# Wider pad tiles, another term order in the out projection, and three projection chunks issued ahead of the layer's sums

## Chip, core and metric

The kernel runs on one core of a Trainium2 chip. The metric is the device time of one execution in microseconds (us), as the median of several executions.

## What is computed

The input x has 512 tokens of 1024 channels. Two blocks of two layers each follow one another; all is float32. Cut to what matters:

```python
def hybrid_layer(x, ...):                        # block 1, twice
    proj = rmsnorm(x, norm_g) @ w_in             # 1024 -> 3584, split in 15 parts
    y_a = conformer_conv(a_u, a_v, ...) * silu(a_z)    # 31 taps, then layer norm
    y_b = short_gated_conv(b_b, b_c, b_x, conv_b_w) * silu(b_z)
    y_c = window_gqa(c_q, c_k, c_v, swa_sink) * silu(c_z)
    y_d = neighborhood_attn(d_q, d_k, d_v, na_rpb) * silu(d_z)
    return x + concat(y_a, y_b, y_c, y_d) @ w_out
x = rms_norm(x, final_norm_g)
for l in range(2):                               # block 2
    proj = rms_norm(x, g_mix) @ w_in             # pool, q, kv, lru and gate parts
    x = x + (g0 * pool + g1 * mla + g2 * lru) @ w_out   # each branch has its projection
    x = x + square(relu(rms_norm(x, g_ffn) @ w_ff1)) @ w_ff2   # 1024 -> 4096 -> 1024
return rms_norm(x, g_final)
```

## The kernel before

Activations lie transposed: a tile is 128 channels by 512 tokens, and x is eight such tiles. Every product with a weight matrix is made in chunks of 128 output channels. `weights` (line 136) loads a chunk (128 x 1024) by DMA on SP's queue into one of two raw tiles and splits it into a high part whi (ACT, line 125) and a low part wlo (DVE, line 126), each with three buffers, so that the split runs up to two chunks ahead of PE. The activations are split in the same way (xh and xl, hh and hl, fh and fl, yh and yl), and `mm3` (line 148) adds three products for each of the eight 128-channel terms: high by high (line 152), high by low (153) and low by high (154). A chunk is so 24 matmuls of 512 columns. `gemm` (line 156) takes a PSUM bank for it from the tag mm, which has three; the attention has banks of its own, two with tag sc for the scores and one with tag o for the output; the remaining two, tag t, serve transposes, sums (ss) and spreads (sp).

The RMS norm is put off: the chunks are made of x times the norm's weights, and the factor R (a token's reciprocal root) is multiplied in when DVE drains a bank (lines 330 to 333, names cq, ck, cv, av, au, kl, ql, kr, qr). R itself comes in a chain: the squares of x's eight tiles are added up (sqa, line 231), PE sums them over the channels (ss, line 169), DVE makes the root in some fourteen steps on 128x4 numbers (lines 175 to 193), spreads it to two diagonal tiles dh and dl (lines 197 and 199), PE multiplies these by ones (sp, lines 200 and 201) and ACT copies R out of the bank (rstd, line 203). No drain of a layer's first projection can start before that. At the end of block 1 there are two such factors: R, and R1, by which DVE multiplies the eight tiles of x (lines 645 and 646). In block 2 the two key and value chunks (kl) and the three query chunks (ql) have norms of their own (Rk and Rq, lines 694 and 700), by the same chain.

What the SBUF pool lays out stands in the order of first use, each tag in as many buffers as it names: the weights, x, hl, work and small tiles first, then three pad tiles (used by the convolutions, the pooling and the LRU part), and behind them hc (the convolution's sums), prob and pth (attention) and sixteen gate tiles. The split activations xh, hh, yh and wfh are hl tiles; fh and fl, the FFN's hidden part, and mh and ml, the merged branches, are gate tiles.

In each engine the instructions stand in an order that the Tile scheduler sets when the program is built, from the order of the code and its own estimate of what is ready; each engine then goes through its own list and waits where an operand isn't there yet. In the layers of block 1, `Side.beside` (line 377) puts the projections between the steps of the attention, and two of the 30 taps of each of two convolutions with every step. The out projection (lines 624 to 633) makes eight chunks over y[0] to y[7], in this order of terms; y[0] and y[1] (`finish_a`, line 593) are the last to be done, as they wait for the layer norm behind the taps. The mixing projection of block 2 (line 882), the two FFN products (lines 897 and 907) and the last projection (line 940) have the same form; in the last, fh is the stationary operand and wfh and wfl the moving ones.

The lines that the change touches, as they stand before:

```python
625            p = gemm(g["w_out"][l, m], y)
...
635        v1 = mean_eps(token_sums(sq.parts()), D)
...
916            R = rstd_of(sq.parts(), D)
```

## Time and profile before

| | us |
|---|---|
| median of 3 executions | 1956.35 |
| lowest and highest | 1953.57, 1956.74 |
| profiled execution | 1955.09 |
| its span in the trace | 1953.3 |

| engine | busy us | share of the span |
|---|---|---|
| PE (matmul) | 1905.2 | 98% |
| DVE | 1208.0 | 62% |
| ACT | 831.7 | 43% |
| POOL | 68.6 | 4% |

The profiled execution takes 1.8 us more than its span, before the first and behind the last recorded instruction. PE is a pipeline, so the duration of one matmul (some 390 ns) overlaps the next; what a matmul costs is read from start to start. The clock that TensorE was granted is shown as a share of full speed, 1.00 for 2.4 GHz and 0.50 for 1.2 GHz.

### The profile page before, as it was taken

To read this page: it belongs to the slowest core of one execution; us is meant where nothing else is said; L and a number is where in the kernel's file an instruction comes from. 1 tells how busy PE (TensorE), PEld (TensorE's weight loads), DVE (VectorE), ACT (ScalarE), POOL (GpSimd) and SP (SyncE) were. 2 spreads that over 40 slices of the span, in tenths; PEclk is the share of its full clock that TensorE was granted. 3 is DMA by queue.
4 is the path that set the end of the run, shared out by engine and by line. 5 is a ranking of instruction groups with operands and counts; after the bars stand their busy time and mean duration, and the time that the engine had idled before them with its cause. 6 is when DMAs were issued, how large, how long until landed. Compare 5 with 4: busy or idle time off the path is not lost.

```text
span 1953.3 us, 23068 instructions
## 1 busy us (share of the span) xinstructions
PE 1905.2 (98%) x8866; PEld 1526.3 (78%) x8866; DVE 1208.0 (62%) x2127; ACT 831.7 (43%) x1343; POOL 68.6 (4%) x83
## 2 busy tenths in 40 slices
PE   7999999999998999999999999999999999999998
PEld 6887778877776788888888888766788888888886
DVE  8997579976787545564444446786455564444454
ACT  7565355654367533343232234367433343323242
POOL 0000100002100000020000001000000010000001
PEclk9999999999999999999999999999999999999999
DMA  5232231222212123323333233221133323333341
GB/s 193 75 97 82 93 102 65 95 76 88 79 58 69 65 87 97 96 88 98 97 96 95 91 97 98 75 79 65 65 97 97 96 87 97 97 92 97 92 129 44
DMA packets 53678, 175.21 MB, mean 90 GB/s; under 512 B 6208, under 2 KB 10176, under 8 KB 53568
## 3 DMA queue, kind: packets, MB, share of 16 engines
q1 hardware_dynamic: 53568, 173.74, 28.1%
q8 instruction: 70, 1.15, 0.2%
q14 instruction: 40, 0.33, 0.1%
HBM read 171.62 MB, written 2.10 MB: 89 GB/s over the span
## 4 chain that ended last, share of the span: by engine, by line
PE 90%; ACT 4%; DVE 4%; issue 2%; DMA 0%; SPq 0%; ACTq 0%; DVEq 0%
PE mm L152 25%; PE mm L153 25%; PE mm L154 25%; PE o L315 2%; PE t L235 2%; PE br L154 1%; PE br L153 1%; PE br L152 1%; PE sc L745 1%; PE sc L440 1%; ACT whi L125 1%; DVE wlo L126 1%; PE last L154 1%; PE last L153 1%; PE last L152 1%
## 5 line engine op out<-in xcount | busy, mean ns | idle before, releaser
L125 ACT ACTIVATE whi<-raw 128x1024 fp32r<-128x1024 f32 (+2 forms) x314 | 320.9, 1023 | 798.6 <-PE mm L153 596.8
L126 DVE TENSOR_TENSOR wlo<-raw,whi 128x1024 fp32r<-128x1024 f32 (+2 forms) x314 | 369.2, 1176 | 169.6 <-ACT whi L125 168.8
L152 PE MATMUL mm<-xh,whi 128*128 128x512 f32 x992 | 396.4, 400 | 9.7 <-ACT whi L125 8.7
L154 PE MATMUL mm<-xh,wlo 128*128 128x512 f32 x992 | 393.7, 397 | 2.3 <-DVE wlo L126 2.2
L153 PE MATMUL mm<-xl,whi 128*128 128x512 f32 x992 | 392.8, 396 | 0.0
L152 PEld LDWEIGHTS mm<-xh,whi 128*128 128x128 f32 x992 | 187.5, 189 | 51.6 <-ACT whi L125 10.8
L154 PEld LDWEIGHTS mm<-xh,wlo 128*128 128x128 f32 x992 | 187.4, 189 | 44.3 <-DVE wlo L126 4.9
L153 PEld LDWEIGHTS mm<-xl,whi 128*128 128x128 f32 x992 | 187.7, 189 | 39.0 <-issue 3.3
L153 PE MATMUL mm<-hl,whi 128*128 128x512 f32 x512 | 199.4, 390 | 0.0
L152 PE MATMUL mm<-hh,whi 128*128 128x512 f32 x512 | 199.2, 389 | 0.0
L154 PE MATMUL mm<-hh,wlo 128*128 128x512 f32 x512 | 199.2, 389 | 0.0
L154 PE MATMUL mm<-fh,wlo 128*128 128x512 f32 x448 | 177.0, 395 | 0.0
L152 PE MATMUL mm<-fh,whi 128*128 128x512 f32 x448 | 176.9, 395 | 0.0
L153 PE MATMUL mm<-fl,whi 128*128 128x512 f32 x448 | 176.9, 395 | 0.0
L909 DVE TENSOR_TENSOR ff<-mm,rstd 128x512 f32<-128x512 f32 x56 | 38.8, 692 | 148.3 <-PE mm L154 148.3
L152 PEld LDWEIGHTS mm<-hh,whi 128*128 128x128 f32 x512 | 96.1, 188 | 20.0
L154 PEld LDWEIGHTS mm<-hh,wlo 128*128 128x128 f32 x512 | 96.1, 188 | 19.9
L153 PEld LDWEIGHTS mm<-hl,whi 128*128 128x128 f32 x512 | 96.1, 188 | 19.9
L332 DVE TENSOR_TENSOR lg<-mm,rstd 128x512 f32<-128x512 f32 x48 | 33.1, 690 | 126.8 <-PE mm L154 126.7
L154 PEld LDWEIGHTS mm<-fh,wlo 128*128 128x128 f32 x448 | 84.1, 188 | 20.4
L153 PEld LDWEIGHTS mm<-fl,whi 128*128 128x128 f32 x448 | 84.1, 188 | 20.4
L152 PEld LDWEIGHTS mm<-fh,whi 128*128 128x128 f32 x448 | 84.1, 188 | 20.3
(302 smaller groups left out, 2754.4 us busy)
## 6 DMA issues: line engine op xcount, KB each, us to landing
raw<-in_w_in SPq DMA_DIRECT2D x124, 512.0 KB, 3.3
raw<-in_w_ff SPq DMA_DIRECT2D x120, 512.0 KB, 3.6
raw<-in_w_out SPq DMA_DIRECT2D x32, 512.0 KB, 3.4
raw<-in_w_br SPq DMA_DIRECT2D x16, 512.0 KB, 3.6
raw<-in_w_last SPq DMA_DIRECT2D x8, 512.0 KB, 3.8
raw<-in_w_q SPq DMA_DIRECT2D x12, 192.0 KB, 2.3
x<-in_xT SPq DMA_DIRECT2D x8, 256.0 KB, 6.6
bends<-in_rpb SPq DMA_DIRECT2D x8, 256.0 KB, 4.5
```

Of the source, the lines that this page charges most:

```text
L125: A.activation(hi, src, AF.Copy)
L126: V.tensor_tensor(lo, src, hi.bitcast(F32), op=ALU.subtract)
L152: T.matmul(out, lhsT=wh, rhs=xh, start=(first and i == 0), stop=False)
L153: T.matmul(out, lhsT=wh, rhs=xl, start=False, stop=False)
L154: T.matmul(out, lhsT=wl, rhs=xh, start=False, stop=(last and i == n - 1))
L235: T.matmul(out, lhsT=in_, rhs=ident, is_transpose=True, start=True, stop=True)
L315: T.matmul(out[64 * j : 64 * j + 64, i * P : (i + 1) * P], lhsT=v(b), rhs=t[:, at[j, e]], start=(b == keys[i][0]), stop=(b == keys[i][1] - 1))
L332: V.tensor_tensor(t, p, R, op=ALU.mult)
L440: T.matmul(out, lhsT=q[j][:, i * P : (i + 1) * P], rhs=k[j][part][:, b0 * P : b1 * P], start=(part == 0), stop=(part == 1))
L745: T.matmul(out, lhsT=q[h][:, i * P : (i + 1) * P], rhs=kt[h][:, b0 * P : b1 * P], start=True, stop=True)
L909: V.tensor_tensor(t, p, Rf2, op=ALU.mult)
```

## The change

1. The pad tiles have 576 columns in place of 542 (seven places in the code, of which the diff shows two); what is written and read of them stays, but the two memsets behind the data in `conv_a`'s part now cover 49 columns instead of 15.
2. The out projection of block 1 adds its terms in the order y4, y5, y2, y6, y7, y3, y0, y1.
3. At the end of both layers of block 1 and of the first layer of block 2, a new function `ahead` issues three chunks of the next layer's projection before the sums that R needs. Their banks are the two of tag sc and the one of tag o, which the attention doesn't use then. The first two chunks are made of the first seven terms each and then of their last one, as x's last tile is the last to be done. `proj` takes these banks where the chunks are asked for: CQ, CQ + 1 and CK in block 1, the two kl chunks and the first ql chunk in block 2.
4. The sums and the root for the FFN's norm (Rf2) move from ahead of the FFN loop to behind its second chunk.

```diff
@@ -153,13 +153,25 @@
             T.matmul(out, lhsT=wh, rhs=xl, start=False, stop=False)
             T.matmul(out, lhsT=wl, rhs=xh, start=False, stop=(last and i == n - 1))
 
-    def gemm(dram, xs):
+    def gemm(dram, xs, order=None):
 
         kk = len(xs)
         h, l = weights(dram, kk, P)
         out = mmps()
-        mm3(out, [((h[:, k, :], l[:, k, :]), xs[k]) for k in range(kk)])
+        mm3(out, [((h[:, k, :], l[:, k, :]), xs[k]) for k in order or range(kk)])
         return out
+
+    def ahead(drams, xs, banks):
+
+        outs = [bank() for bank in banks]
+        ws = [weights(d, KD, P) for d in drams[:2]]
+        for ks in (range(KD - 1), range(KD - 1, KD)):
+            for out, (h, lo) in zip(outs, ws):
+                for k in ks:
+                    mm3(out, [((h[:, k, :], lo[:, k, :]), xs[k])], k == 0, k == KD - 1)
+        h, lo = weights(drams[2], KD, P)
+        mm3(outs[2], [((h[:, k, :], lo[:, k, :]), xs[k]) for k in range(KD)])
+        return outs
 
     def token_sums(parts):
 
@@ -483,7 +495,7 @@
             t = work("avt")
             A.activation(t, v, AF.Tanh, scale=0.5)
             u = scaled(proj(AU + c), R, "au")
-            pad = ap_.tile([P, S + 30], F32, tag="pad", name=uniq("pad"), bufs=3)
+            pad = ap_.tile([P, S + 64], F32, tag="pad", name=uniq("pad"), bufs=3)
             G.memset(pad[:, :15], 0.0)
             G.memset(pad[:, S + 15 :], 0.0)
             V.scalar_tensor_tensor(pad[:, 15 : S + 15], t, 1.0, u, op0=ALU.add, op1=ALU.mult)
@@ -622,7 +634,7 @@
         sqf = SumSq() if last else None
         nxs = []
         for m in range(KD):
-            p = gemm(g["w_out"][l, m], y)
+            p = gemm(g["w_out"][l, m], y, (4, 5, 2, 6, 7, 3, 0, 1))
             V.scalar_tensor_tensor(x[m], p, 0.5, x[m], op0=ALU.mult, op1=ALU.add)
             sq.add(x[m])
             if last:
@@ -632,6 +644,8 @@
             else:
                 nxs.append(split_tile(x[m], col("norm_g", l + 1, m), "x"))
         xs = nxs
+        cs = (CQ, CQ + 1, CK) if not last else (5, 6, 2)
+        first = dict(zip(cs, ahead([g["w_in_2"][0, c] if last else g["w_in"][l + 1, c] for c in cs], xs, (scps, scps, ops))))
         v1 = mean_eps(token_sums(sq.parts()), D)
         if not last:
             R = spread(rsqrt(v1))
@@ -680,7 +694,7 @@
         bd = {(n, c): bdt[:, 2 * i + c, :] for i, n in enumerate(HEADED) for c in range(2)}
 
         def proj(c):
-            return gemm(g["w_in_2"][l, c], xs)
+            return first.pop(c) if c in first else gemm(g["w_in_2"][l, c], xs)
 
 
         cos, sin = gate("cos"), gate("sin")
@@ -883,11 +897,8 @@
             V.scalar_tensor_tensor(x[m], p, 0.5, x[m], op0=ALU.mult, op1=ALU.add)
             sq.add(x[m])
             hs.append(split_tile(x[m], col("g_ffn_2", l, m), "h"))
-        rf = rsqrt(mean_eps(token_sums(sq.parts()), D))
-        V.tensor_tensor(rf, rf, rf, op=ALU.mult)
-        Rf2 = spread(rf)
-
-
+
+        sums = sq
         sq = SumSq()
         nxs = []
         last = l == DEPTH - 1
@@ -901,6 +912,10 @@
                 hi, lo = gate("fh", dt=F32R), gate("fl", dt=F32R)
                 split(t, hi, lo)
                 f.append((hi, lo))
+                if qt == 0 and c == 1:
+                    rf = rsqrt(mean_eps(token_sums(sums.parts()), D))
+                    V.tensor_tensor(rf, rf, rf, op=ALU.mult)
+                    Rf2 = spread(rf)
             if last and qt == 3:
                 break
             for m in range(KD):
@@ -913,12 +928,13 @@
                     nxs.append(split_tile(x[m], col("g_mix_2", l + 1, m), "x"))
         if not last:
             xs = nxs
+            first = dict(zip((5, 6, 2), ahead([g["w_in_2"][l + 1, c] for c in (5, 6, 2)], xs, (scps, scps, ops))))
             R = rstd_of(sq.parts(), D)
 
 
     gf = []
     for h in range(2):
-        t = ap_.tile([P, S + 30], F32, tag="pad", name=uniq("gf"), bufs=3)[:, :S]
+        t = ap_.tile([P, S + 64], F32, tag="pad", name=uniq("gf"), bufs=3)[:, :S]
         nc.sync.dma_start(out=t, in_=g["g_final"][:, h * S : (h + 1) * S].to_broadcast([P, S]))
         gf.append(t)
     ss = small("ssh")
```

The scheduler makes of this other lists for the engines. Four places follow, before and then after (a line of after stands 12 to 16 lower in its file than the same line of before). PE, start of layer 0's out projection; yh_1949 and yl_1950 are y0, yh_1991 and yl_1992 are y1, mm_2001, mm_2039 and mm_2077 the first three chunks. Before:

```order
L152 MATMUL mm_2077<-yh_1949,whi_2073 128x512
L153 MATMUL mm_2077<-yl_1950,whi_2073 128x512
L154 MATMUL mm_2077<-yh_1949,wlo_2074 128x512
L152 MATMUL mm_2001<-yh_1991,whi_1997 128x512
L152 MATMUL mm_2039<-yh_1991,whi_2035 128x512
L152 MATMUL mm_2077<-yh_1991,whi_2073 128x512
L153 MATMUL mm_2001<-yl_1992,whi_1997 128x512
L154 MATMUL mm_2001<-yh_1991,wlo_1998 128x512
L152 MATMUL mm_2001<-yh_1206,whi_1997 128x512
```

After:

```order
L152 MATMUL mm_2001<-yh_1907,whi_1997 128x512
L153 MATMUL mm_2001<-yl_1908,whi_1997 128x512
L154 MATMUL mm_2001<-yh_1907,wlo_1998 128x512
L152 MATMUL mm_2001<-yh_1949,whi_1997 128x512
L153 MATMUL mm_2001<-yl_1950,whi_1997 128x512
L154 MATMUL mm_2001<-yh_1949,wlo_1998 128x512
L152 MATMUL mm_2001<-yh_1991,whi_1997 128x512
L153 MATMUL mm_2001<-yl_1992,whi_1997 128x512
L154 MATMUL mm_2001<-yh_1991,wlo_1998 128x512
```

The terms of y0 and y1 came ahead of the others of their chunk, with three chunks open at once; now they close each chunk, and one chunk is done before the next begins.

PE, start of layer 1 of block 1, where the transposes of cv (t_2539) stand; cv's own chunk is mm_2512, mm_2552 is av's, mm_2587 au's and mm_2626 the second av's. Before:

```order
L154 MATMUL mm_2552<-xh_2067,wlo_2549 128x512
L152 MATMUL mm_2552<-xh_2107,whi_2548 128x512
L153 MATMUL mm_2552<-xl_2108,whi_2548 128x512
L235 MATMUL t_2539<-c_ident,cv_2537 128x128 x4
L154 MATMUL mm_2552<-xh_2107,wlo_2549 128x512
L152 MATMUL mm_2552<-xh_2147,whi_2548 128x512
L153 MATMUL mm_2552<-xl_2148,whi_2548 128x512
```

After:

```order
L152 MATMUL mm_2587<-xh_2307,whi_2583 128x512
L153 MATMUL mm_2587<-xl_2308,whi_2583 128x512
L154 MATMUL mm_2587<-xh_2307,wlo_2584 128x512
L247 MATMUL t_2539<-c_ident,cv_2537 128x128 x4
L152 MATMUL mm_2626<-xh_2029,whi_2622 128x512
L153 MATMUL mm_2626<-xl_2030,whi_2622 128x512
```

The transposes stood inside av's chunk, one chunk behind cv's; now they stand behind cv's, av's and au's, which hold all three mm banks, and the chunk that follows takes cv's bank again.

PE, start of block 2; sp_4730 before and sp_4761 after spread Rk. Before:

```order
L152 MATMUL mm_4829<-xh_4405,whi_4825 128x512
L153 MATMUL mm_4829<-xl_4406,whi_4825 128x512
L200 MATMUL sp_4730<-dh_4731,ones_r 128x512
L154 MATMUL mm_4829<-xh_4405,wlo_4826 128x512
L152 MATMUL mm_4829<-xh_4450,whi_4825 128x512
L153 MATMUL mm_4829<-xl_4451,whi_4825 128x512
L201 MATMUL sp_4730<-dl_4732,ones_r 128x512
L154 MATMUL mm_4829<-xh_4450,wlo_4826 128x512
```

After:

```order
L152 MATMUL mm_4921<-xh_4495,whi_4917 128x512
L153 MATMUL mm_4921<-xl_4496,whi_4917 128x512
L181 MATMUL ss_4737<-ones,sqa_4735 128x1 x4
L154 MATMUL mm_4921<-xh_4495,wlo_4918 128x512
L212 MATMUL sp_4761<-dh_4762,ones_r 128x512
L213 MATMUL sp_4761<-dl_4763,ones_r 128x512
L152 MATMUL mm_4969<-xh_4184,whi_4965 128x512
```

The two spreads stood inside a chunk, with its matmuls ahead of and between them; now a single matmul stands between the sums ss_4737 and the spread.

DVE, start of block 2; x_67 to x_74 are x, rstd_4580 and rstd_4673 are R1, kl the two key chunks, and sqa feeds the sums for Rk. Before:

```order
L126 TENSOR_TENSOR wlo_4826<-raw_4823,whi_4825 128x1024
L646 TENSOR_TENSOR x_67<-x_67,rstd_4580 128x512
L646 TENSOR_TENSOR x_68<-x_68,rstd_4580 128x512
L646 TENSOR_TENSOR x_69<-x_69,rstd_4580 128x512
L646 TENSOR_TENSOR x_70<-x_70,rstd_4580 128x512
L646 TENSOR_TENSOR x_71<-x_71,rstd_4580 128x512
L646 TENSOR_TENSOR x_72<-x_72,rstd_4580 128x512
L646 TENSOR_TENSOR x_73<-x_73,rstd_4580 128x512
L646 TENSOR_TENSOR x_74<-x_74,rstd_4580 128x512
L332 TENSOR_TENSOR kl_4700<-mm_4675,rstd_4548 128x512
L126 TENSOR_TENSOR wlo_4918<-raw_4915,whi_4917 128x1024
L231 TENSOR_TENSOR sqa_4704<-sq_4667,sq_4702 128x512
```

After:

```order
L344 TENSOR_TENSOR kl_4731<-sc_4500,rstd_4641 128x512
L660 TENSOR_TENSOR x_67<-x_67,rstd_4673 128x512
L660 TENSOR_TENSOR x_68<-x_68,rstd_4673 128x512
L660 TENSOR_TENSOR x_69<-x_69,rstd_4673 128x512
L660 TENSOR_TENSOR x_70<-x_70,rstd_4673 128x512
L660 TENSOR_TENSOR x_71<-x_71,rstd_4673 128x512
L660 TENSOR_TENSOR x_72<-x_72,rstd_4673 128x512
L660 TENSOR_TENSOR x_73<-x_73,rstd_4673 128x512
L660 TENSOR_TENSOR x_74<-x_74,rstd_4673 128x512
L243 TENSOR_TENSOR sqa_4735<-sq_4729,sq_4733 128x512
```

The eight multiplications by R1 stood between the two kl drains; now they stand behind both and ahead of sqa.

## Rows read from the trace of the kernel before

**Rows 1.** The page, part 1: busy us (share of the span) xinstructions, by engine.

```profile
PE 1905.2 (98%) x8866; PEld 1526.3 (78%) x8866; DVE 1208.0 (62%) x2127; ACT 831.7 (43%) x1343; POOL 68.6 (4%) x83
```

**Rows 2.** Groups by line: line, engine, operation, out<-in, xcount | busy us, mean ns.

```profile
L152 PE MATMUL mm<-hh,whi 128*128 128x512 f32 x512 | 199.2, 389 | 0.0
...
L154 PE MATMUL mm<-fh,wlo 128*128 128x512 f32 x448 | 177.0, 395 | 0.0
...
L154 PE MATMUL mm<-mh,wlo 128*128 128x512 f32 x128 | 50.6, 395 | 0.0
```

**Rows 3.** Timeline of PE (start us, us) where fh begins, hh begins, fh begins.

```profile
914.71 0.40 PE L152 MATMUL mm<-fh,whi 128*128 128x512 f32 x1
...
959.50 0.39 PE L152 MATMUL mm<-hh,whi 128*128 128x512 f32 x1
...
1003.03 0.40 PE L152 MATMUL mm<-fh,whi 128*128 128x512 f32 x1
```

**Rows 4.** PE's waits: who waited for whom: us in total, times, longest us.

```profile
PE ss L169 <- DVE sqa L231: 4.3, 2, 3.3
```

**Rows 5.** Timeline of PE, start of the out projections of layer 0 and 1 (idle in brackets).

```profile
208.21 0.39 PE L152 MATMUL mm<-yh,whi 128*128 128x512 f32 x1
...
210.60 0.50 PE L154 MATMUL mm<-yh,wlo 128*128 128x512 f32 x1 [0.42 <-DVE wlo L126]
212.59 1.03 PE L152 MATMUL mm<-yh,whi 128*128 128x512 f32 x3 [1.49 <-ACT yh L125]
...
213.90 0.63 PE L154 MATMUL mm<-yh,wlo 128*128 128x512 f32 x1
214.32 0.63 PE L152 MATMUL mm<-yh,whi 128*128 128x512 f32 x1
...
455.39 0.49 PE L154 MATMUL mm<-yh,wlo 128*128 128x512 f32 x1 [0.42 <-DVE wlo L126]
457.38 0.97 PE L152 MATMUL mm<-yh,whi 128*128 128x512 f32 x3 [1.50 <-ACT yh L125]
```

**Rows 6.** Busy time by stretch: us, PE, PEld, DVE, ACT, POOL (xcount), PEclk, DMA share, GB/s.

```profile
213.40:216.80 3.40, 3.40 (x9) 2.71 (x9) 0.00 (x0) 0.00 (x0) 0.00 (x0) 0.50 0.00 0
506.90:513.80 6.90, 6.90 (x21) 5.75 (x22) 3.33 (x15) 1.06 (x1) 0.00 (x0) 0.51 0.07 29
296.00:386.00 90.00, 89.91 (x493) 73.26 (x493) 87.28 (x171) 54.23 (x118) 0.25 (x3) 1.00 0.27 87
```

**Rows 7.** Timeline of DVE, PE and ACT at the layer end of block 1.

```profile
256.05 0.69 DVE L626 SCALAR_TENSOR_TENSOR x<-mm,x 128x512 f32<-128x512 f32 x1 [1.60 <-PE mm L154]
...
264.23 1.22 DVE L126 TENSOR_TENSOR wlo<-raw,whi 128x1024 fp32r<-128x1024 f32 x1
...
292.78 0.69 DVE L332 TENSOR_TENSOR au<-mm,rstd 128x512 f32<-128x512 f32 x1 [3.30 <-PE mm L154]
...
258.94 1.02 PE L169 MATMUL ss<-ones,sqa 128*128 128x1 f32 x8
...
282.99 0.66 PE L235 MATMUL t<-c_ident,cv 128*128 128x128 f32 x4 [1.56 <-DVE cv L332]
...
264.90 0.60 ACT L203 ACTIVATE rstd<-sp 128x512 f32<-128x512 f32 x1 [1.36 <-PE sp L201]
...
269.69 5.14 ACT L247 ACTIVATE rot<-cq 32x512 f32<-32x512 f32 x8
```

**Rows 8.** Timeline of ACT and DVE at the end of block 1.

```profile
517.80 0.60 ACT L203 ACTIVATE rstd<-sp 128x512 f32<-128x512 f32 x1 [4.55 <-PE sp L201]
...
522.23 4.89 DVE L646 TENSOR_TENSOR x<-x,rstd 128x512 f32<-128x512 f32 x8
...
560.64 0.69 DVE L332 TENSOR_TENSOR qr<-mm,rstd 128x512 f32<-128x512 f32 x1 [2.06 <-PE mm L154]
```

**Rows 9.** Timeline of DVE at the layer end of block 2.

```profile
1234.59 0.69 DVE L332 TENSOR_TENSOR kl<-mm,rstd 128x512 f32<-128x512 f32 x1
...
1277.57 0.69 DVE L332 TENSOR_TENSOR qr<-mm,rstd 128x512 f32<-128x512 f32 x1
```

More of the change, by code (lines that the diff above doesn't have):

```diff
@@ L551, in conv_b @@
             cb = scaled(proj(BC + c), R, "bc")
-            pad = ap_.tile([P, S + 30], F32, tag="pad", name=uniq("padb"), bufs=3)
+            pad = ap_.tile([P, S + 64], F32, tag="pad", name=uniq("padb"), bufs=3)
             G.memset(pad[:, :1], 0.0)
@@ L759, in pool @@
         def pool(c):
-            pu = ap_.tile([P, S + 30], F32, tag="pad", name=uniq("padp"), bufs=3)
+            pu = ap_.tile([P, S + 64], F32, tag="pad", name=uniq("padp"), bufs=3)
             G.memset(pu[:, :16], 0.0)
@@ L768, in pool @@
             while w < wins[1]:
-                nxt = ap_.tile([P, S + 30], F32, tag="pad", name=uniq("padd"), bufs=3)
+                nxt = ap_.tile([P, S + 64], F32, tag="pad", name=uniq("padd"), bufs=3)
                 G.memset(nxt[:, :16], 0.0)
@@ L791, in lru_in @@
         def lru_in(c):
-            pu = ap_.tile([P, S + 30], F32, tag="pad", name=uniq("padl"), bufs=3)
+            pu = ap_.tile([P, S + 64], F32, tag="pad", name=uniq("padl"), bufs=3)
             G.memset(pu[:, :3], 0.0)
@@ L812, in lru_in @@
             A.activation(tr, tr, AF.Tanh)
-            a2 = ap_.tile([P, S + 30], F32, tag="pad", name=uniq("a2"), bufs=3)[:, :S]
+            a2 = ap_.tile([P, S + 64], F32, tag="pad", name=uniq("a2"), bufs=3)[:, :S]
             A.activation(a2, a, AF.Square)
```

## The prediction

> **What bounds the kernel now.** I read the page first: PE is busy 98% of the span, 1905.2 of 1953.3 us, and no other engine two thirds of it [rows 1]. So the time is the sum of PE's matmuls plus the few stretches in which PE stands still or runs at the lower clock, and a change can only pay in three ways: a cheaper matmul, a wait less, a clock drop less. Next I looked at what one matmul costs [rows 2], then start to start in time order [rows 3], since a duration of 389 ns overlaps the next one: the 192 matmuls of one FFN quarter over hh, hl run from 959.50 to 1003.03, 226.7 ns each; the 192 over fh, fl from 914.71 to 959.50, 233.3 ns each. The shape, the weights' tiles and the clock are the same. Then PE's waits [rows 4]; by places the largest that the change touches are the two out projections of block 1 [rows 5], the layer end of block 1 [rows 7] and the end of block 1 (3.3 us [rows 4]). Last I looked at the granted clock by stretches [rows 6]: after some of these waits PE is granted 0.50, the 1.2 GHz level. A matmul then takes 427 ns start to start (213.90 to 214.32 [rows 5]), so the 3.4 us stretch costs 3.4 x (1 - 227/427) = 1.6 us and a 6.8 us stretch 3.2 us.
>
> **Wider pads.** The pads' contents are the same, and the reads of them too. What moves is what the pool lays out behind them. Three pads of 542 floats take 3 x 2176 bytes (rounded up), 25.5 times 256; so gate, hc, prob and pth tiles, which come later, start at a multiple of 256 bytes, while whi, wlo, hl, work and x start 128 bytes off one. Three pads of 576 floats take 27 times 256, and all start 128 off. The rows split just so: matmuls that pair a weight tile with an hl tile (hh) have a mean of 389 ns, those that pair one with a gate tile (fh, mh) 395 [rows 2]; the last projection pairs fh and wfh, a gate and an hl tile, in the same way. Whether the distance of the two operands decides or where the one starts, the new layout puts every pair where the fast ones stand, and I take 226.7 ns for all. One quarter is worth 44.79 - 43.53 = 1.26 us [rows 3]. There are 7 quarters over fh (3 x 448 matmuls), mh and ml make 2 more (3 x 128), the last projection 1 (3 x 64): 10 x 1.26 = **12.6 us**. Bounds: 0 if the place in memory is not the cause, 12.6 if it is wholly; I take the upper, because the step at 914.71 and back at 959.50 falls on the very matmul where the tile changes. The four memsets that grow from 15 to 49 columns are on POOL, which is 4% busy [rows 1]: 0.
>
> A rule of the Trainium skill speaks against this part. Its page "TensorE: Matmul & The Clock Gate" (section "Step-by-step: what each phase is for") says that PE reads the moving operand and the next weights through two read ports that don't take bandwidth from each other, so the tile that is streamed should not matter, this term would be 0 and the sum 1958.9 us. The trace does not agree as it stands: 6.6 ns per matmul go with the tile and with nothing else that I find [rows 3].
>
> **Order of the out projection.** y0 and y1 end last: zz of y1 is split into yh and yl on ACT and DVE while PE has started [rows 5]. Before, PE took the y0 terms of three chunks, waited 0.42 for the third chunk's wlo and 1.49 for y1, and was then granted half the clock. After, six finished terms come first: 18 matmuls x 0.227 = 4.1 us from 208.21, so y0 is wanted at 212.3 and y1 at 213.0; the yh that ended the wait let PE go at 212.59, and yl is read one matmul later. The work stays the same, the waits are covered by these 18 matmuls; without them they would be back. Layer 0: 0.42 + 1.49 + 1.6 = 3.5; layer 1, without a drop behind its waits, 0.42 + 1.50 = 1.9 [rows 5]. Together **5.4 us**, between 5.0 (a rest of 0.2 each for yl) and 5.4.
>
> **Three chunks ahead of the sums.** These 72 matmuls (16.3 us) are put before ss, the sums that R hangs on. PE is busy meanwhile, but R comes later by about that, and then every drain of the next layer (cq, ck, cv, av: they multiply by R) comes later, while PE has only its three mm banks to go on with, 16.3 us less what ss and sp take.
>
> Layer end of block 1. Before, the last chunk's drain starts at 256.05, ss at 258.94, and R is done at 265.50, 6.6 us behind ss [rows 7]. After, ss starts at 256.05 + 16.3 = 272.4, and the R chain on DVE has a split of weights (wlo, 1.2 us [rows 7]) standing in its middle: R at about 280.1, 14.6 us later. PE works through cv, av, au until 290.8 (with a wait of 0.7 at sp). The transposes of cv come next in its order, and cv's drain stands on DVE behind the rope work of cq and ck, whose copies are 12 x 0.64 us on ACT [rows 7], with four splits and a weight split between them: 280.8 + 5.1 + 2.6 + 2.6 + 1.1, then two DVE steps, 293.6. PE waits 2.8, against 1.56 before: 0.7 + 2.8 - 1.6 = 1.9 worse at the start of attention. DVE carries more: after cv its work is 10.7 us later (293.6 against 282.9), 1.7 of it done earlier, 3.5 absorbed by its idle time at 289 to 293 [rows 7], so 5.5 left; and in the next 90 us it is 97% busy, 87.28 of 90 [rows 6], as it has the convolution's taps to do beside the drains. That is a stretch in which DVE is as tight as PE. Between 1.9 and 9.0 (the whole backlog), I take the middle of 1.9 and 5.5, rounded up: **-4**.
>
> End of block 1. Before: 3.3 idle, a clock drop (3.2), and 1.0 at the sums for Rq behind it [rows 4, 6]: 7.5 us to be won. After: PE is busy to 515.4, two groups of sums to 517.2, then three chunks to about 535. R comes at 525.1 (518.4 before [rows 8]), R1 at 529.7; on DVE the loop of eight x times R1 (4.89 us [rows 8]) now stands ahead of sqa, so the sums for Rk end at about 536.3 and dh is done at 541.0, where before PE had a chunk to fill this. PE stands from about 536.5 to 541.0, and a bit more for ql's drain: some 5.5, most of what was won. By my replay qr's chunk, whose drain was at 560.64 [rows 8], is 0.6 us later without a drop and 3.8 with one; I take **-2**.
>
> Layer end of block 2. Before, PE runs through there almost without a wait, so there is nothing to win. After: ss stands 72 matmuls later, but before it had been let in among a chunk's matmuls, so R comes 14.2 us later, at about 1248.7 (the first drain that needs it started at 1234.59 [rows 9]), Rk and Rq behind it in turn; three short waits at sp (0.3 to 0.6) and one for qr, whose drain moves from 1277.57 [rows 9] to about 1279.5: **-2** (0 to -5).
>
> **FFN sums two chunks later.** PE has no wait at ss there before, and Rf2 is first read in the first drain of ff2, six chunks after the new place: 0. On SP one weight load changes place by two rows, and the weights are split two chunks ahead of PE: 0.
>
> **The sum.** 12.6 + 5.4 - 4 - 2 - 2 = 10.0 us. The profiled execution took 1955.09 us (span 1953.3): 1945.1. The median of the three runs is 1.26 us above it: **1946.4 us**. A measurement of this kernel tells about 0.2% from no change, 3.9 us: below 1952.4 is faster, above 1960.3 slower.
>
> **Rivals.** (1) The new waits are followed by half clock at the layer ends (not all were before: the one that ends at 282.99 wasn't, the 3.3 us one at the end of block 1 was [rows 4, 6, 7]): 1.6 to 3.2 each at two places, 5 us: 1951.4, on the line between faster and same. (2) The place in memory isn't the cause of 233 ns, but something in the stage, as what DVE and ACT write meanwhile: 5.4 - 8 = -2.6, 1958.9, same. For it: no row of before shows a gate tile at another place. Against it: the step up and the step back fall on the very matmuls where the tile changes [rows 3]. (The rule of the page named above would give this case.) (3) The layer ends work as drawn and PE finds work all the time: 12.6 + 5.4 + 1.6 + 7.5 = 27.1, 1929.3. Against it: three banks hold 16.3 us, and from ss to the first drain that frees one it is over 20 at the first layer end. (4) Slower: the late R goes through to PE. R is 14.6, 6.7 and 14.2 us later at the three places, 35.5 in all; my replay lets 8 of them reach PE. If more than 22 did (18 won + 3.9), the kernel would be slower; all of it gives 1946.4 + 27.5 = 1973.9. For it: DVE 97% busy behind the first place. Against: three whole chunks more are done by then, so what PE has left behind each R is 16.3 us less.
>
> **Chances.** Forecast 0.62 (1941 to 1952); rival 1 0.12, half of it faster; rival 2 0.10; rival 3 0.08; rival 4 0.08. Faster 0.62 + 0.06 + 0.08 = 0.76, same 0.10 + 0.06 = 0.16, slower 0.08. The range leaves out rivals 3 and 4: 1936 (a layer end that costs nothing) to 1959 (rival 2).
>
> **What would show it.** Right: mm from fh and mh at 389 ns, 192 of them in 43.5 us; no idle at 210 and 455, no drop at 213; new waits at cv's transposes near 291, at sp and the chunk behind it near 537 to 543; qr of block 2's second layer a little later. Wrong: fh still at 395; PE idle or half clock over 5 us at one layer end; DVE filled to 100% up to 400 with PE waiting for z or sc drains in between.

## The result, and the profile after

The changed kernel takes **1940.73 us** (median of 4 runs, 1938.73 to 1942.16) against 1955.62 for the kernel before beside it (4 runs, 1953.57 to 1956.74): a ratio of 0.9924 with a 95% interval from 0.9907 to 0.9942. That is 14.9 us faster, where the prediction said 10.0; the time lies inside its range (1936 to 1959), 5.7 us under its value and 0.3 below the 1941 to 1952 that it held likeliest. The profiled execution's span went from 1953.3 to 1939.4 us.

The changed file's line numbers are 12 to 16 higher, as said above. The first part of the page has PE at 98% of the span still, with 13.9 us less of busy time in the same 8866 instructions, as much as the span lost, so the gain is in what matmuls cost and PE's idle time is no less in all [rows 1]:

```profile
PE 1891.3 (98%) x8866; PEld 1525.1 (79%) x8866; DVE 1204.1 (62%) x2127; ACT 831.8 (43%) x1343; POOL 68.2 (4%) x83
```

Groups by line show where. The matmuls over fh and mh now cost what those over hh cost [rows 2]:

```profile
L152 PE MATMUL mm<-hh,whi 128*128 128x512 f32 x512 | 199.2, 389 | 0.0
...
L154 PE MATMUL mm<-fh,wlo 128*128 128x512 f32 x448 | 174.3, 389 | 0.0
...
L154 PE MATMUL mm<-mh,wlo 128*128 128x512 f32 x128 | 49.8, 389 | 0.0
```

In PE's timeline, the quarter over fh, fl (first two rows) and the quarter over hh, hl (second and third) both take 43.52 us; before it was 44.79 and 43.53 [rows 3]:

```profile
911.26 0.39 PE L152 MATMUL mm<-fh,whi 128*128 128x512 f32 x1
...
954.78 0.39 PE L152 MATMUL mm<-hh,whi 128*128 128x512 f32 x1
...
998.30 0.39 PE L152 MATMUL mm<-fh,whi 128*128 128x512 f32 x1
```

PE at the start of layer 0's out projection: from 208.47 on nothing stands in brackets, so PE waits neither for the split of the weights nor for y1, whose first matmul is at 213.23. The rows at 210.60 and 212.59 of before have no counterpart [rows 5], and none is there in layer 1:

```profile
208.47 0.39 PE L152 MATMUL mm<-yh,whi 128*128 128x512 f32 x1
...
212.55 0.39 PE L152 MATMUL mm<-yh,whi 128*128 128x512 f32 x1
...
213.23 0.39 PE L152 MATMUL mm<-yh,whi 128*128 128x512 f32 x1
```

The layer ends cost something instead. At the layer end of block 1 (PE, then ACT, then DVE) ss starts at 268.60, R is done at 276.26, and the transposes of cv wait 2.90 us, against 1.56 before [rows 7]. The weights' split of 1.23 us at 270.47 stands between ss and R:

```profile
268.60 0.94 PE L181 MATMUL ss<-ones,sqa 128*128 128x1 f32 x8
...
289.89 1.09 PE L247 MATMUL t<-c_ident,cv 128*128 128x128 f32 x4 [2.90 <-DVE cv L344]
...
275.66 0.60 ACT L215 ACTIVATE rstd<-sp 128x512 f32<-128x512 f32 x1 [6.03 <-PE sp L213]
...
270.47 1.23 DVE L126 TENSOR_TENSOR wlo<-raw,whi 128x1024 fp32r<-128x1024 f32 x1
...
289.06 0.68 DVE L344 TENSOR_TENSOR cv<-mm,rstd 128x512 f32<-128x512 f32 x1
```

At the end of block 1 (PE, then DVE) the loop of eight x times R1 starts at 524.80 and takes 4.91 us, sqa comes behind it, and the sp matmul behind that waits 4.04 us. Then ql's drain costs 0.40 and qr's 1.23:

```profile
530.81 0.95 PE L181 MATMUL ss<-ones,sqa 128*128 128x1 f32 x8
...
536.14 0.77 PE L212 MATMUL sp<-dh,ones_r 128*128 128x512 f32 x1 [4.04 <-DVE dh L209]
...
538.03 0.79 PE L152 MATMUL mm<-xh,whi 128*128 128x512 f32 x1 [0.40 <-DVE ql L344]
...
558.42 0.50 PE L152 MATMUL mm<-qh,whi 128*128 128x512 f32 x1 [1.23 <-DVE qr L344]
...
524.80 4.91 DVE L660 TENSOR_TENSOR x<-x,rstd 128x512 f32<-128x512 f32 x8
529.63 0.68 DVE L243 TENSOR_TENSOR sqa<-sq,sq 128x512 f32<-128x512 f32 x1
```

At the layer end of block 2 the sums stand at 1232.22 without a wait, and two short waits follow, for the sums of Rk and for qr:

```profile
1232.22 0.95 PE L181 MATMUL ss<-ones,sqa 128*128 128x1 f32 x8
...
1255.03 1.02 PE L181 MATMUL ss<-ones,sqa 128*128 128x1 f32 x8 [0.54 <-DVE sqa L243]
...
1270.58 0.50 PE L152 MATMUL mm<-qh,whi 128*128 128x512 f32 x1 [1.89 <-DVE qr L344]
```

Busy time by stretch (PE, PEld, DVE, ACT, POOL, then the granted clock): around the end of both new waits and behind it PE is granted the 1.2 GHz level, and DVE in the 90 us behind the first layer end is about as busy as before [rows 6].

```profile
289.40:292.80 3.40, 2.91 (x9) 2.56 (x10) 3.36 (x6) 3.30 (x7) 0.00 (x0) 0.50 0.00 0
535.20:541.90 6.70, 5.36 (x11) 3.67 (x12) 5.94 (x15) 3.94 (x7) 1.23 (x1) 0.50 0.00 1
296.00:386.00 90.00, 89.97 (x502) 73.14 (x501) 85.98 (x170) 55.06 (x119) 0.24 (x3) 1.00 0.28 92
```

### The profile page after: what moved, and what is told of

It reads as the page before. It is cut to its first block, busy times and chain, and to the rows that moved or that the text cites. A ratio compares the mean times of both kernels' runs of the same rounds, so it can differ in the third digit from the quotient of the medians.

```text
span 1939.4 us, 23050 instructions
## 1 busy us (share of the span) xinstructions
PE 1891.3 (98%) x8866; PEld 1525.1 (79%) x8866; DVE 1204.1 (62%) x2127; ACT 831.8 (43%) x1343; POOL 68.2 (4%) x83
## 4 chain that ended last, share of the span: by engine, by line
PE 72%; DVE 3%; ACT 2%; issue 1%; DVEq 0%; ACTq 0%
PE mm L152 19%; PE mm L153 19%; PE mm L154 19%; PE br L154 1%; PE br L152 1%; PE br L153 1%; PE sc L759 1%; PE o L327 1%; PE t L247 1%; PE last L154 1%; PE last L152 1%; PE last L153 1%; PE ss L181 0%; ACT whi L125 0%; ACT p L296 0%
## 5 line engine op out<-in xcount | busy, mean ns | idle before, releaser
L152 PE MATMUL mm<-xh,whi 128*128 128x512 f32 x920 | 369.1, 402 | 10.2 <-ACT whi L125 8.8
L154 PE MATMUL mm<-xh,wlo 128*128 128x512 f32 x920 | 365.6, 397 | 2.3 <-DVE wlo L126 2.3
L153 PE MATMUL mm<-xl,whi 128*128 128x512 f32 x920 | 364.7, 396 | 0.0
L152 PEld LDWEIGHTS mm<-xh,whi 128*128 128x128 f32 x920 | 174.4, 190 | 49.8 <-ACT whi L125 10.9
L154 PEld LDWEIGHTS mm<-xh,wlo 128*128 128x128 f32 x920 | 173.9, 189 | 41.4 <-DVE wlo L126 4.9
L153 PEld LDWEIGHTS mm<-xl,whi 128*128 128x128 f32 x920 | 174.2, 189 | 36.1 <-issue 3.3
```

Source lines behind the costliest of these rows:

```text
L152: T.matmul(out, lhsT=wh, rhs=xh, start=(first and i == 0), stop=False)
L153: T.matmul(out, lhsT=wh, rhs=xl, start=False, stop=False)
L154: T.matmul(out, lhsT=wl, rhs=xh, start=False, stop=(last and i == n - 1))
```

## The experiments

Each kernel ran beside the kernel before on the same chip. "The gain" is the difference of the two medians. A kernel with no ratio has one run, in which only differences of several us mean anything.

**The pads alone.** The kernel before with S + 64 in place of S + 30 at all seven places, and nothing else.

```diff
-            pad = ap_.tile([P, S + 30], F32, tag="pad", name=uniq("pad"), bufs=3)
+            pad = ap_.tile([P, S + 64], F32, tag="pad", name=uniq("pad"), bufs=3)
```

> The kernel before with pads of 576 columns and nothing else. Theory of the place (gate tiles 128 bytes off a multiple of 256, as the weights): the mean of a matmul over fh or mh falls from 395 to 389 ns, a quarter of 192 matmuls from 44.8 to 43.5 us, ten such groups, about 12.4 us off the time (ratio 0.9937). Rival, load of the stage (what DVE and ACT write meanwhile): no change, 395 ns stays, and the whole gain of the changed kernel comes from its order.

Measured: 1942.04 us against 1953.68, a ratio of 0.9941 [0.9925, 0.9958]; the gain is 11.6. The matmuls over fh and mh have a mean of 389 ns (the line over mh shown above for the changed kernel stands word for word in this one's profile). Added up in the timeline, nine quarters of 192 went from 44.79 to 43.52 us and the last projection from 48.04 to 47.12: 9 x 1.27 + 0.92 = 12.4 us. So the pads' width alone brings most of the change's gain. It leaves open why, since wider pads also change the memsets and the distances inside the pads.

**Is it the place of the tiles, and which place?** Three kernels with the pads of before. In the first, an unused tile of 128 bytes is allocated behind the pads, so only the tiles behind it move; in the second it has 64 bytes; in the third 128 bytes stand ahead of everything, so that both kinds of tiles move and their distance stays: the weights and hl tiles then start at a multiple of 256 bytes, the gate tiles 128 off it. (The places are worked out from the tiles' sizes in the code; the traces show no addresses.)

```diff
+            if l == 0 and c == 0:
+                G.memset(ap_.tile([P, 32], F32, tag="gap", name="gap", bufs=1), 0.0)
             acc = ap_.tile([P, S], F32, tag="hc", name=uniq("hc"), bufs=2)
```

```diff
-                G.memset(ap_.tile([P, 32], F32, tag="gap", name="gap", bufs=1), 0.0)
+                G.memset(ap_.tile([P, 16], F32, tag="gap", name="gap", bufs=1), 0.0)
```

```diff
+    G.memset(cst.tile([P, 32], F32, name="gap"), 0.0)
     ones = cst.tile([P, 1], F32, name="ones")
```

> Pads stay 542 columns wide; an unused tile of 128 bytes is laid out behind them, so the tiles behind start 128 bytes off a multiple of 256 as with wide pads. If the place decides: as with wide pads, 389 ns over fh and mh and about 12.4 us off. If the width of the pads decides: 395 ns, no change.

> The same with 64 bytes: gate tiles start 64 off a multiple of 256, the weights 128 off one. If any difference of the two starts costs 6.6 ns per matmul: 395 ns over fh and mh, no change in time. If only a difference of 128 does: 389 ns and 12.4 us off. Something between is possible too.

> Pads of 542 columns; an unused tile of 128 bytes ahead of everything, so that weights, x and hl tiles start at a multiple of 256 and gate tiles 128 off: the difference of before, with the places exchanged. If the difference of the two operands decides: 395 ns over fh, 389 over hh, no change in time. If the start of the streamed tile alone decides (0 slow, 128 fast): 389 over fh, 395 over hh, xh and yh, the time up by some 20 us (3 x 992 + 3 x 512 + 3 x 128 matmuls get 6.6 ns, 32 us, less the 12.4).

Measured, one run each: 1944.38, 1953.35 and 1952.97 us, spans 1942.6, 1951.6 and 1951.2 (1939.3 for wider pads). The first is 3.3 us longer than with wider pads because PE has the half clock, from 212.15 and from 457.91 for 3.4 us each, behind waits in the two out projections that both kernels have; what that costs is worked out with the order of the terms below. The groups by line, of the three kernels in turn, for the matmuls over hh and over fh. With 128 bytes behind the pads, fh costs 389 ns as hh does:

```profile
L152 PE MATMUL mm<-hh,whi 128*128 128x512 f32 x512 | 199.2, 389 | 0.0
...
L152 PE MATMUL mm<-fh,whi 128*128 128x512 f32 x448 | 174.3, 389 | 0.0
```

With 64 bytes behind them, fh costs 394:

```profile
L152 PE MATMUL mm<-hh,whi 128*128 128x512 f32 x512 | 199.5, 390 | 0.0
...
L152 PE MATMUL mm<-fh,whi 128*128 128x512 f32 x448 | 176.7, 394 | 0.0
```

With 128 bytes ahead of all, fh costs 395, though its tiles stand now where hl's stood, and hh, whose tiles stand where the gate tiles stood, costs 390 (line numbers are one higher here):

```profile
L153 PE MATMUL mm<-hh,whi 128*128 128x512 f32 x512 | 199.4, 390 | 0.0
...
L153 PE MATMUL mm<-fh,whi 128*128 128x512 f32 x448 | 177.0, 395 | 0.0
```

So it is the place and not the pads' width: 128 bytes that nobody reads behind them give the same matmul. And it is no property of one tile's start, as the exchange of places changes nothing. What is left is the difference between the start of the weights' tile and that of the streamed tile, modulo 256 bytes. Where a gate tile is streamed, 0 costs 226.7 ns from matmul to matmul, 128 and 64 cost about 233, and half the distance doesn't halve the price (a quarter over fh takes 44.80 us with 64 bytes). In the last projection, where the gate tile fh is the stationary operand and an hl tile is streamed, it is otherwise: 64 bytes cost 0.27 us there and 128 cost 0.92, as its 192 matmuls take 47.39 us with 64 bytes (first start to last end), 47.12 with none and 48.04 with 128:

```profile
1895.25 0.48 PE L152 MATMUL last<-wfh,fh 128*128 128x512 f32 x1
...
1942.24 0.40 PE L154 MATMUL last<-wfh,fl 128*128 128x512 f32 x1
```

So it matters too which of the two operands starts behind the other, or which is the stationary one; no run parts these. The rule of the Trainium skill that the prediction weighed (its page "TensorE: Matmul & The Clock Gate", section "Step-by-step: what each phase is for"), that the two reads take no bandwidth from each other, agrees here only with the tiles of equal remainders (226.7 ns); for the others the measurement decides. Why the chip does so no run shows.

**The order of the terms alone.** The kernel before with the new order in block 1's out projection.

```diff
-        mm3(out, [((h[:, k, :], l[:, k, :]), xs[k]) for k in range(kk)])
+        mm3(out, [((h[:, k, :], l[:, k, :]), xs[k]) for k in order or range(kk)])
...
-            p = gemm(g["w_out"][l, m], y)
+            p = gemm(g["w_out"][l, m], y, (4, 5, 2, 6, 7, 3, 0, 1))
```

> The kernel before with the new order of terms in the out projection and nothing else. By the sum: 3.5 in layer 0 (with its clock drop) and 1.9 in layer 1, 5.4 us; the trace of the kernel without ahead has also 0.9 less wait at the end of block 1: 4.8 (no drop to lose) to 6.3 us, ratio 0.997 to 0.9975. If the rest that the kernel without ahead gained beyond the pads (about 10 us by medians) came from the order alone: 0.995.

Measured: 1947.00 us against 1954.13, a ratio of 0.9959 [0.9945, 0.9974]; the gain is 7.1, somewhat over the 4.8 to 6.3 expected. The waits at both out projections are gone, 0.42 + 1.49 + 0.42 + 1.50 = 3.8 us [rows 5]. There was something at the end of block 1 too that the prediction did not have: the wait for the sums, 3.26 us at 505.88 in before, is 2.35 us here:

```profile
499.97 1.02 PE L169 MATMUL ss<-ones,sqa 128*128 128x1 f32 x8 [2.35 <-DVE sqa L231]
```

DVE sets the pace there: in before it drains one chunk into x each 5.88 us (479.41, 485.29), while PE needs 5.44 for one, and in the old order three chunks were open at once, so the first drain came late (462.99, now 456.16). That is 0.9 more. Most of the rest is clock. In before PE is granted 0.50 from 213.37 for 3.4 us and from 506.91 for 6.8 [rows 6]; here not at all at the first place, and for 3.4 us, from 502.84, at the second. What 3.4 us of half clock cost among these matmuls shows without a formula: from the first matmul over yh to the first over xh, layer 0's out projection takes 47.64 us in before and 46.03 with the pads alone, which has the same two waits (at 210.52 and 212.51) and the full clock behind them:

```profile
213.00:216.50 3.50, 3.50 (x17) 2.79 (x16) 0.18 (x1) 0.00 (x0) 0.00 (x0) 1.00 0.04 18
```

That is 1.6 us, as the prediction's formula has it, and 3.2 for the two places. But this part is not bound to the order: in the five kernels with the old order (before and the four above) the same pair of waits stands ten times, in two layers each, and half clock follows four of them.

**The three chunks ahead.** The changed kernel without the three calls of `ahead`, where the chunks and sums stand as before; and the changed kernel with the one at the end of block 1 kept.

```diff
-        first = dict(zip(cs, ahead([...], xs, (scps, scps, ops))))
...
-            first = dict(zip((5, 6, 2), ahead([...], xs, (scps, scps, ops))))
```

```diff
-        first = dict(zip(cs, ahead([...], xs, (scps, scps, ops))))
+        if last:
+            first = dict(zip(cs, ahead([...], xs, (scps, scps, ops))))
...
-            first = dict(zip((5, 6, 2), ahead([...], xs, (scps, scps, ops))))
```

> The changed kernel without its three calls of ahead (pads, term order and later FFN sums stay). If the layer ends lose on the whole, as predicted (8 us) and as the two traces suggest (1.6 + 2.3 + 0.8 = 4.7 us by places): 4.7 us faster than the changed kernel, about 1936, ratio to before 0.990. If ahead pays on the whole: slower than the changed kernel, 1943 or more.

> The same with ahead kept at the end of block 1 alone. If its price there is the idle time at the spread of Rk (4.0 us) against the 3.3 us of idle and the clock drop that it removes: within 2 us of the kernel without ahead, rather slower (about 1937 to 1938). If ahead pays where PE did stand idle before: 3 to 6 us faster than without (1931 to 1933).

> The changed kernel again, on the chip of the three others, as their measure: 1940.7 us, ratio to before 0.9924.

Measured on one chip: 1932.87 us without `ahead` (ratio 0.9890 [0.9877, 0.9904]), 1936.18 with the one at the end of block 1 (0.9907 [0.9893, 0.9920]), and 1940.21 for the changed kernel itself (0.9928 [0.9915, 0.9942]). So the chunks ahead cost 7.3 us: 3.3 at the end of block 1 (where up to about 2 was expected), 4.0 at the two layer ends. By the stages of the two traces (a table below) it is 1.7 from layer 0's out projection to layer 1's, 4.4 from there to block 2's first matmul over mh and 1.5 to the second layer's, 7.5 together. The spans are 8.4 apart; 0.9 of that lies ahead of layer 0's out projection, where no chunk has been issued ahead yet, so it isn't theirs. PE's waits without `ahead`, at the layer end of block 1 and at the end of block 1:

```profile
278.49 0.66 PE L247 MATMUL t<-c_ident,cv 128*128 128x128 f32 x4 [1.55 <-DVE cv L344]
...
498.18 1.02 PE L181 MATMUL ss<-ones,sqa 128*128 128x1 f32 x8 [2.34 <-DVE sqa L243]
...
537.29 1.02 PE L181 MATMUL ss<-ones,sqa 128*128 128x1 f32 x8 [1.01 <-DVE sqa L243]
...
553.60 0.50 PE L152 MATMUL mm<-qh,whi 128*128 128x512 f32 x1 [0.78 <-DVE qr L344]
```

The cv wait is 1.55 again, as before the change, and at the end of block 1 PE waits 2.34 + 1.01 + 0.78 in place of 4.04 + 0.40 + 1.23 in the changed kernel. No single wait is large; the chunks ahead replace waits by others of the same kind.

**What makes the wait at the end of block 1?** Two causes stood in the prediction together: R comes late, and the loop of x times R1 stands ahead of sqa on DVE. The first experiment moves the sums and R between the first 42 matmuls of the three chunks and the rest, so that R comes sooner and PE has work behind ss; the loop keeps its place ahead of sqa. The second keeps the sums behind the chunks and writes the loop later in the program.

```diff
                 for k in ks:
                     mm3(out, [((h[:, k, :], lo[:, k, :]), xs[k])], k == 0, k == KD - 1)
+            if sums and len(ks) > 1:
+                got = sums()
```

```diff
-            for m in range(KD):
-                V.tensor_tensor(x[m], x[m], R1, op=ALU.mult)
...
+        if l == 0:
+            for m in range(KD):
+                V.tensor_tensor(x[m], x[m], R1, op=ALU.mult)
         kr = scaled(proj(7), R, "kr")
```

> As the former, but both sums and R come in the middle of ahead, after the first seven terms of two chunks (42 matmuls, 9.5 us) in place of after three chunks (16.3 us). If the late R makes the wait at the spread of Rk: that wait shrinks from 4 us to under 1, no drop of the clock behind it, 3 to 6 us faster than with the sums last. If the loop x times R1 alone makes it: the wait stays at 3 to 4 us and the time within 1.5 us.

> Ahead kept at the end of block 1 alone, sums last, as in the run of that kind; the loop x times R1 is written behind the norms of kl and ql, and the scheduler puts two of its eight steps ahead of sqa in place of all. If the loop on DVE is what the spread of Rk waits for: sqa comes 6 x 0.6 = 3.7 us earlier, the wait of 4.0 us falls under 1, no clock drop behind it, and the time falls by 3 to 7 us against the same kernel with the loop ahead (1936.2 to about 1931). If the late R alone makes the wait: it stays at 3 us or more.

With the sums in the middle: 1933.43 us (ratio 0.9891 [0.9877, 0.9904]), 2.8 less than the kernel that it starts from (3 to 6 were expected) and as fast as the one without `ahead`. PE and DVE at the end of block 1:

```profile
525.64 0.95 PE L183 MATMUL ss<-ones,sqa 128*128 128x1 f32 x8
...
531.30 0.47 PE L214 MATMUL sp<-dh,ones_r 128*128 128x512 f32 x1 [0.24 <-DVE dh L211]
...
534.18 0.47 PE L152 MATMUL mm<-xh,whi 128*128 128x512 f32 x1 [1.48 <-DVE ql L346]
...
538.98 1.02 PE L183 MATMUL ss<-ones,sqa 128*128 128x1 f32 x8 [0.68 <-DVE sqa L245]
...
518.04 4.90 DVE L666 TENSOR_TENSOR x<-x,rstd 128x512 f32<-128x512 f32 x8
```

ss comes at 525.64 in place of 530.81, the wait at sp falls from 4.04 to 0.24 us with no half clock behind it, and 1.48 and 0.68 come up. The loop (518.04, 4.90 us) is still ahead of sqa as a whole, and from ss to dh it takes as long as in the kernel that it starts from (4.7 us, dh at 530.29, against 4.3). But 19 matmuls stand between ss and sp in place of one. So the loop alone doesn't make the wait; that no work of PE is left between ss and sp does. The edit also brings the sums themselves sooner, and no run parts the two.

With the loop written later: 1936.71 us (0.9906 [0.9891, 0.9921]), no gain, and the wait at sp is 3.41 us. By the words of the expectation that would make the late R alone the cause, but DVE's timeline tells why the run says little:

```profile
534.05 0.47 PE L212 MATMUL sp<-dh,ones_r 128*128 128x512 f32 x1 [3.41 <-DVE dh L209]
...
523.29 1.29 DVE L720 TENSOR_TENSOR x<-x,rstd 128x512 f32<-128x512 f32 x2
524.50 0.69 DVE L243 TENSOR_TENSOR sqa<-sq,sq 128x512 f32<-128x512 f32 x1
...
526.74 0.68 DVE L720 TENSOR_TENSOR x<-x,rstd 128x512 f32<-128x512 f32 x1
...
529.43 0.69 DVE L720 TENSOR_TENSOR x<-x,rstd 128x512 f32<-128x512 f32 x1
...
533.04 0.86 DVE L209 TENSOR_SCALAR dh<-c_ident,yh 128x128 fp32r<-128x128 f32 x4
```

The scheduler put two of the eight multiplications ahead of sqa, one behind it (525.10) and five between the first step on the sums and dh (from the row at 526.74 to the one at 529.43), so they are in the way still: sqa starts 2.3 us sooner than in the kernel that it starts from (526.79), but from the first step on the sums to dh it takes 6.4 us (526.66 to 533.04) in place of 3.3. What the loop costs on its own this run doesn't tell.

**Both, and neither chunks nor loop.** The sums in the middle with the loop written later; and the kernel without `ahead` with the loop written later (both edits as above).

> Sums in the middle of ahead at the end of block 1, and the loop x times R1 late. If the two causes add: the waits of 1.5 (bank of ql) and 0.7 (sums for Rq) shrink too, some 1 to 2 us faster than with the sums in the middle alone, about 1932. If DVE's work is only moved: the waits move to ql and qr, same time.

> The kernel without ahead, with the loop x times R1 late. PE's waits there at the end of block 1 are 2.3 (sums), 0.3, 1.0 and 0.8. If the loop stands in any of them: the last two shrink, 1 us or so faster, 1932. If not: the same 1932.9.

Measured: 1931.53 us (0.9881 [0.9865, 0.9898]) and **1931.41** (0.9880 [0.9865, 0.9894]), both near the 1932 expected. Both beat the changed kernel, with intervals that don't touch its 0.9907 to 0.9942, and don't differ from each other; the second, simpler one is the fastest here. In the first the wait for ql's bank is gone, but that for the sums for Rq has grown, from 0.68 to 1.26 us. The second's two waits for sums at the end of block 1:

```profile
497.93 1.02 PE L181 MATMUL ss<-ones,sqa 128*128 128x1 f32 x8 [2.35 <-DVE sqa L243]
...
532.71 1.02 PE L181 MATMUL ss<-ones,sqa 128*128 128x1 f32 x8 [0.31 <-DVE sqa L243]
```

The second wait is 0.31 us in place of 1.01 in the kernel without `ahead`, and qr's of 0.78 is gone. By medians, and on different chips, the later loop is worth 1.5 us, which the two intervals don't separate.

## Why the prediction was right, and where it was off

**Wider pads: 12.6 said, 12.4 measured** in the traces, 11.6 by the medians. The step that held was the reading of the start to start times, with the step up and the step back on the matmul where the tile changes [rows 3]. The small rest is the last projection, which brought 0.92 where the prediction put the 1.26 of the other groups. The prediction left open whether the distance or the start decides, and didn't need it; the exchange of places shows the distance. Rival 2, that the place is not the cause, falls with the 128-byte tile.

Where PE's stages begin in each profiled execution shows the other parts: the first matmul over yh in layers 0 and 1 of block 1, over mh in layers 0 and 1 of block 2, and the first over xh behind each of the first three (us from the span's start; worked out from PE's timeline).

| kernel | yh, 0 | xh | yh, 1 | xh | mh, 0 | xh | mh, 1 | span |
|---|---|---|---|---|---|---|---|---|
| before | 208.21 | 255.85 | 452.99 | 499.06 | 824.57 | 1224.48 | 1540.87 | 1953.3 |
| changed | 208.47 | 252.28 | 450.99 | 494.79 | 822.59 | 1215.90 | 1533.12 | 1939.4 |
| order alone | 209.35 | 253.15 | 450.27 | 494.06 | 817.10 | 1216.98 | 1533.35 | 1945.8 |
| changed, no chunks ahead | 207.58 | 251.36 | 448.44 | 492.27 | 815.61 | 1208.92 | 1524.69 | 1930.9 |

**Order of the terms: 5.4 said, 7.1 measured** by the medians, and 8.6 by the table from layer 0's yh on: 3.8 and 2.3 from yh to xh, 2.5 from there to block 2's mh. This is the term that was mis-sized. The two waits, 3.8 of it, came as worked out. Two things were wrong in the rest. The 1.6 us of half clock behind the wait at 212.59 is no sure consequence of it, as the same waits come with and without it. And the 2.5 behind the block's end (0.9 less wait for the sums and 3.4 us less of half clock) were overlooked, because the part of the prediction on the order ended with PE's own waits and did not follow DVE to the layer's end.

**Chunks ahead: -8 said, -7.3 measured** against the kernel without them, -7.5 by the table. That these agree is in part luck. The prediction's -4, -2 and -2 are set against before; taken so, the three stages behind xh are 1.6, 2.3 and 0.8 us longer, 4.7 together. Between the two counts lie 2.8 us: without the chunks these stages are 0.1, 2.2 and 0.6 shorter than before, most of it what the order wins behind block 1, which the prediction had nowhere.

At the layer end of block 1 the replay was good: ss, R and cv's drain were said for 272.4, 280.1 and 293.6, and came at 268.60, 276.26 and 289.06, all about 4 us sooner, which is what the order of terms had won by then (47.64 to 43.81 us from yh to xh); the wait at cv is 2.90 where 2.8 was said. But the second half of that term, DVE's backlog that would reach PE in the next 90 us, did not come: from 291 to 411 the trace has no wait of PE, with DVE at 85.98 of 90 us busy. So this place cost 1.6 us and not 4, and that with the half clock that came around the end of the wait. It would have been 3 without a piece of luck: the wait of 1.64 us at 427.59 in before is 0.22 in the changed kernel and in its repeat, and 1.64 in every other. These two are the only ones with chunks ahead at this layer end, and PE's list is another there: the attention's matmuls stand in smaller groups, with three matmuls of a chunk between two of them (from 426.63).

At the end of block 1 the new wait was said to be 5.5 us from 536.5 on, a bit of it for ql's drain; it is 4.04 to 536.14 and 0.40 behind. Half clock of 6.8 us came around it (the prediction took the middle between with and without). By the prediction's own list, half clock of over 5 us at a layer end was a sign of being wrong; but before has 6.8 us of it there too. The stage from layer 1's yh to block 2's first mh takes as long as before (371.6 us in both), so all that the order wins there is lost: without the chunks the stage takes 367.2, with the order alone 366.8. At block 2's layer end qr's wait came as said (1.89 us), and the price is 0.8 against before and 1.5 against the kernel without chunks, where -2 was said.

**The sum.** The medians of the parts make 11.6 + 7.1 - 7.3 = 11.4; the change measured 14.9 (14.5 in the repeat). The intervals of these ratios are 5 to 7 us wide, so the medians don't resolve a difference of 3.5. The traces nearly close it. From layer 0's yh to the end the changed kernel takes 14.2 us less than before; pads 12.4, order 8.6, chunks -7.5 and the FFN's sums 0.4 make 13.9. (The first FFN quarter of each of the two layers is 0.2 us shorter with the later sums; no run tries that edit by itself, and its 0 is nearly right.) Ahead of layer 0's yh lie 207.3 to 209.7 us in the fourteen profiled executions, 208.5 and 209.0 for the changed kernel and its repeat; a part of what the medians show is that spread.

**Rivals.** Half clock behind the new waits (rival 1) did come, at three places (3.4 us from 289.37, 6.8 from 535.13, 3.4 from 559.03), but half clock elsewhere went or shrank: up to PE's last matmul it is 23.9 us in the profiled execution of before, 20.5 in that of after and 23.9 in that of the repeat. Rival 3 (PE finds work all the time) is off by 11 us, with the waits at 290 and 536 against it, and rival 4 (the late R goes through whole) by 33; against that speaks most the stretch from 291 to 411 without a wait.

## What to carry to other kernels

When the same matmul costs different times over different tiles, compare where the two operands start, modulo 256 bytes, and try an unused 128-byte tile laid out between them before anything else. Work that is put ahead of a reduction keeps an engine busy only if something is left for it after the reduction too: count what stands between the sum and its first reader, as well as what stands ahead. And follow a reordering on the engine that drains to the next place where that engine is the bound, since the gain may come up there.

## What the runs showed of the hardware

Two things were not expected. The first is that price of operand starts: 6.6 ns for each 128x512 matmul over fh or mh whose two operands start 64 or 128 bytes apart modulo 256, as much at the one as at the other, and in the last projection, with the kinds of tiles exchanged, 4.8 ns at 128 bytes and 1.4 at 64; 12.4 us of 1955 in this kernel.

The second is how far the half clock varies from one execution of a program to another. At the start of block 2's attention PE waits 4.0 us in one execution of the changed kernel (to 626.07) and 4.1 in the other (to 625.41). The one has half clock until 630.7, and full clock from 631 on:

```profile
627.30:630.70 3.40, 3.40 (x21) 2.41 (x21) 2.23 (x2) 1.65 (x3) 0.00 (x0) 0.50 0.40 117
631.00:634.00 3.00, 2.98 (x26) 2.22 (x25) 0.91 (x1) 2.03 (x3) 0.00 (x0) 1.00 0.54 187
```

The other, the repeat, has it from 625.0 to 631.6:

```profile
625.00:628.00 3.00, 2.59 (x10) 1.58 (x12) 2.53 (x6) 3.00 (x5) 0.00 (x0) 0.50 0.00 0
628.40:631.60 3.20, 3.20 (x21) 2.64 (x17) 1.15 (x1) 0.70 (x2) 0.00 (x0) 0.50 0.74 229
```

The stretch is 3.4 us in the one and 6.8 in the other, from the same program and about the same wait. By the formula of the prediction, which held among the back-to-back matmuls of the out projection, that would make 1.6 us; here, among the attention's, the time from the end of the wait to the first matmul over mh is 196.5 and 197.2 us, 0.7 apart. So a clock drop that one trace shows behind a wait is a poor price for that wait.
